# Moving the mixers' GpSimd element work, and one LN affine, to VectorE in a four-layer kernel

## The chip, the cores and the metric

The kernel runs on one core of one Trainium2 chip. A core has a matrix engine (TensorE, PE in the views; its weight loads are shown as PEld), three engines for element work (VectorE = DVE, ScalarE = ACT, GpSimd = POOL), and SyncE (SP), which here only issues transfers. The metric is the device time of one execution in microseconds (us), as a median of several runs. Each engine takes its instructions in order; an instruction that has to wait for another engine or a transfer holds up what stands behind it on its own engine.

## The reference

The input is 256 tokens of 1024 fp32 values. Two hybrid layers come first, then two blocks that each have a mixer and a mixture of experts (MoE). Cut to what matters:

```
def hybrid_layer(x, ...):                 # called twice
    p = rmsnorm(x, norm_g) @ w_in         # 3488 columns
    q, k, v   = low-rank attention inputs, rmsnorm per head, rope
    o_a       = causal attention(q, k, v)
    o_b       = c_b * short_conv(c_c * c_h, conv_w)
    o_c       = sg_u * (w_s @ layernorm(sg_v) + b_s)
    o_d       = second causal attention, rmsnorm per head, rope
    y = concat([o_a*silu(g_a), o_b*silu(g_b), o_c*silu(g_c), o_d*silu(g_d)])
    return y @ w_out                      # added to x by the caller

def second_block(x, c, ...):
    for i in range(2):                    # i = 0: NA, i = 1: GQA
        sh1, sc1, g1, sh2, sc2, g2 = split(silu(c) @ ada_w[i] + ada_b[i])
        y = (neighbourhood_mixer, gqa_mixer)[i](x * (1 + sc1) + sh1)
        x = layer_norm(ALPHA * x + (1 + g1) * y, ln_g[i, 0], ln_b[i, 0])
        y = hierarchical_moe(x * (1 + sc2) + sh2)
        x = layer_norm(ALPHA * x + (1 + g2) * y, ln_g[i, 1], ln_b[i, 1])
    return x
```

## The kernel before

**Stages.** The program runs through hybrid layer 0, hybrid layer 1, the NA layer, the MoE of block 0, the GQA layer and the MoE of block 1. In the profiled execution these are about 0 to 165, 165 to 330, 330 to 495, 495 to 945, 945 to 1100 and 1100 to 1560.8 us. In the MoE stages weights stream through a ring of buffers; in the mixers (hybrid, NA, GQA) the weights are few and products many.

**Products in three.** A mixer's projection is not one fp32 product but three on values split in two parts (`mm3`, L177): each weight block is split by `split` (L117), per 128x1024 piece, into hi, a ScalarE copy (L125), and lo = v - hi (L128). In the kernel before, lo is made on VectorE or on GpSimd: every third piece goes to GpSimd by the string `SPLIT_ON_POOL`, and in two calls of `proj_wide`, the first projection of a hybrid layer (`wa`) and GQA's `wkv`, the parameter `e` sends the others there too. There are two halves of the hi and lo blocks, used in turn, so a piece can be split only when the products from two blocks earlier have read theirs.

**Row norms.** `rstd` (L180) makes 1/sqrt by a bit trick and three Newton steps. The scale (L191) and the seed (L192) are VectorE's; the steps (L194 to L202) are GpSimd's in a hybrid layer, 13 instructions, and VectorE's in GQA, 10 instructions, since there the last two of a step are one (L199). A hybrid layer calls it for `r3` (the low-rank inputs; L507 reads it), `rb` (the second attention's heads; L524), `rq` (the first attention's heads; L543 to L545) and `rv` (the spatial gate; L587).

**Other element work on GpSimd.** In a hybrid layer: a gain on the keys (L552), half of a gain (L569), the gate's gain, bias and mask (L588 to L590). In `mixer_out`, which closes NA and GQA: router weights (L787). In GQA: the rope tables (L903, 16 small ones) and the rope of the second half of the queries (`chain` with `e=G`, L931 to L938).

**The affine between the layers.** The MoE of block 0 ends with the normalised x; gain and bias of that layer norm are folded into GQA's input scale (`fold`), and x itself gets them later, by four instructions on 128x1024 (`affine`, L840), since `mixer_out` adds it to the mixer's output. They run on GpSimd behind the k and v projection; their rows come by transfer into block 6 early in the layer.

**The adaptive scales.** `ada_cols` computes silu(c) @ ada_w in 24 pieces, each a product of 16 instructions into a bank of its own (`pf`), a copy of that bank (L220 or L226, tile `parts`), a second small product, and a VectorE instruction (L723, tile `modc`). Pieces are put between the mixers' steps by `ADA_PLAN`, and TensorE cannot start the next before the last has been copied.

**What sets the order.** The program is written as a list of operations with tiles, and a list scheduler with a simulated timeline makes each engine's order from it. An edit to one operation can therefore move many.

## Time and profile before

| | |
|---|---|
| median of 3 runs | 1562.01 us (1561.87 to 1565.7) |
| span of the profiled execution | 1560.8 us |
| TensorE busy | 1231.1 us (79%) |
| VectorE busy | 569.4 us (36%), 1258 instructions |
| ScalarE busy | 356.6 us (23%) |
| GpSimd busy | 236.6 us (15%), 283 instructions |
| DMA, mean | 341 GB/s |

The shares are means over stages of two kinds. In the MoE stages the transfers run near 427 GB/s without a break and the element engines are nearly idle; in the mixers TensorE is 85% to 95% busy, and VectorE and GpSimd do most of their work there. So the mixers have to be read by stretches: the windows by stage first, then what TensorE waited for, then the timeline around each such wait.

### The profile page before, as it was taken

The page shows a single profiled execution, that of the slowest core. Times are in us where ns is not written, and L with a number is a line of the kernel's source. Part 1 is how long each engine was busy: PE and PEld are TensorE (multiplying, and loading weights), DVE is VectorE, ACT ScalarE, POOL GpSimd, SP SyncE. Part 2 cuts the span into 40 slices and gives each one's busy share as a digit, 9 for nine tenths or more (in the row PEclk, how much of TensorE's full clock was granted, in tenths as well). Part 3 has the DMA queues.
Part 4 walks back from the last instruction along what each step waited for, and adds up shares of the span by engine and source line. Part 5 has one row for each costly group of instructions (what it writes and reads, how often), then busy time and mean ns, then how long its engine had stood idle before and what let it go on. Part 6 is the DMA issues. An engine that isn't in the chain of part 4 may idle for free.

```text
span 1560.8 us, 24728 instructions
## 1 busy us (share of the span) xinstructions
PE 1231.1 (79%) x10584; PEld 789.8 (51%) x10584; DVE 569.4 (36%) x1258; ACT 356.6 (23%) x759; POOL 236.6 (15%) x283
## 2 busy tenths in 40 slices
PE   6898899999998986664877768889897764586774
PEld 6787788777967442321333326757543322243322
DVE  6677567555467210100111105877411100011113
ACT  5453443444442100000000004363100000010000
POOL 2721272122111200000000004320200000000000
PEclk9999999999999998876898889989999887798797
DMA  9436543468487999999999999575999999999995
GB/s 370 178 147 242 213 166 152 163 236 343 169 342 290 405 426 427 427 428 426 427 426 427 428 423 410 210 279 206 388 427 427 428 427 425 427 427 427 426 427 210
DMA packets 46705, 532.76 MB, mean 341 GB/s; under 512 B 7040, under 2 KB 10240, under 8 KB 15104
## 3 DMA queue, kind: packets, MB, share of 16 engines
q1 hardware_dynamic: 45440, 527.99, 82.2%
q10 hardware_dynamic: 1152, 3.15, 0.6%
q8 instruction: 85, 1.39, 0.4%
q14 instruction: 28, 0.23, 0.0%
HBM read 530.07 MB, written 1.05 MB: 340 GB/s over the span
## 4 chain that ended last, share of the span: by engine, by line
DMA 43%; PE 40%; DVE 9%; POOL 2%; ACT 2%; issue 2%; SPq 0%; DVEq 0%; ACTq 0%; POOLq 0%
DMA b<-in_moe_w_gate_up_dram 25%; DMA b<-in_moe_w_down_dram 16%; PE ps L162 14%; PE pd L177 9%; PE ps L177 8%; PE pf L162 3%; PE pd L162 3%; PE ps L159 3%; DMA b<-in_ada_w_dram 2%; DVE b L128 1%; ACT b L125 1%; POOL b L128 1%; POOL rs L196 0%; POOL rs L201 0%; DVE b L220 0%
## 5 line engine op out<-in xcount | busy, mean ns | idle before, releaser
L162 PE MATMUL ps<-b,b 128*32 128x256 f32 (+2 forms) x5248 | 484.6, 475 | 198.2 <-DMA b<-in_moe_w_gate_up_dram 138.9
L162 PEld LDWEIGHTS ps<-b,b 128*32 128x32 f32 (+1 forms) x5248 | 191.6, 120 | 432.1 <-issue 275.7
L177 PE MATMUL ps<-b,b 128*128 128x256 f32 (+1 forms) x1464 | 198.8, 295 | 6.6 <-DVE gates L565 5.6
L177 PEld LDWEIGHTS ps<-b,b 128*128 128x128 f32 x1464 | 186.7, 195 | 17.1 <-DVE gates L565 6.1
L177 PE MATMUL pd<-b,b 128*128 128x256 f32 (+2 forms) x1152 | 188.3, 320 | 4.6 <-ACT b L600 1.3
L177 PEld LDWEIGHTS pd<-b,b 128*128 128x128 f32 x1152 | 162.0, 196 | 25.3 <-issue 4.4
L128 POOL TENSOR_TENSOR b<-b,b 128x1024 fp32r<-128x1024 f32 (+2 forms) x46 | 115.5, 2517 | 348.2 <-ACT b L125 348.2
L125 ACT CAST b<-b 128x1024 fp32r<-128x1024 f32 (+1 forms) x124 | 126.1, 1035 | 160.2 <-PE ps L177 71.7
L226 ACT COPY b<-ps 128x256 f32<-128x256 f32 (+1 forms) x81 | 36.0, 449 | 456.4 <-PE ps L162 308.2
L128 DVE TENSOR_TENSOR b<-b,b 128x1024 fp32r<-128x1024 f32 x78 | 115.9, 1490 | 62.1 <-ACT b L125 57.0
L220 DVE COPY b<-ps 128x256 f32<-128x256 f32 (+1 forms) x71 | 36.2, 510 | 263.1 <-PE ps L162 214.1
L1115 POOL TENSOR_TENSOR b<-b,g 128x128 f32<-128x128 f32 x64 | 23.6, 399 | 595.1 <-PE ps L159 548.7
L1097 DVE SCALAR_TENSOR_TENSOR sl<-sl,ps 128x128 f32<-128x128 f32 x64 | 18.4, 288 | 248.4 <-ACT sl L1096 248.4
L159 PE MATMUL ps<-cst,b 128*128 128x128 f32 (+1 forms) x404 | 77.5, 302 | 39.7 <-DVE b L220 17.5
L159 PEld LDWEIGHTS ps<-cst,b 128*128 128x128 f32 (+1 forms) x404 | 45.3, 147 | 105.2 <-DVE b L220 34.7
L162 PE MATMUL pd<-b 64*128 64x512 f32 (+1 forms) x384 | 82.6, 552 | 15.4 <-DVE b L1145 12.9
L1145 DVE TENSOR_TENSOR b<-ps,parts 128x512 f32<-128x512 f32 x32 | 22.1, 692 | 180.8 <-PE ps L162 179.9
L162 PEld LDWEIGHTS ps<-b,x 128*128 128x128 f32 x512 | 68.3, 218 | 21.9 <-issue 18.4
L162 PE MATMUL ps<-b,x 128*128 128x128 f32 x512 | 72.2, 305 | 3.8 <-issue 1.6
L1096 ACT ACTIVATE sl<-ps 128x128 f32<-128x128 f32 x64 | 17.8, 278 | 236.9 <-PE ps L159 236.9
L162 PE MATMUL pf<-b,cact 128*32 128x256 f32 x704 | 56.0, 428 | 13.5 <-DVE modc L723 4.9
L162 PEld LDWEIGHTS pd<-b 64*128 64x128 f32 x384 | 34.3, 190 | 52.9 <-DVE b L1145 26.2
(304 smaller groups left out, 944.0 us busy)
## 6 DMA issues: line engine op xcount, KB each, us to landing
b<-in_moe_w_gate_up_dram SPq DMA_DIRECT2D x128, 2048.0 KB, 32.5
b<-in_moe_w_down_dram SPq DMA_DIRECT2D x62, 2048.0 KB, 35.3
b<-in_ada_w_dram SPq DMA_DIRECT2D x24, 2048.0 KB, 8.4
b<-in_w_in_dram SPq DMA_DIRECT2D x12, 2048.0 KB, 8.0
b<-in_na_w_qkv_dram SPq DMA_DIRECT2D x6, 2048.0 KB, 9.3
b<-in_gqa_w_qkv_dram SPq DMA_DIRECT2D x3, 2048.0 KB, 23.4
b<-in_w_out_dram SPq DMA_DIRECT2D x4, 1024.0 KB, 5.7
b<-in_w_out_dram SPq DMA_DIRECT2D x2, 2048.0 KB, 7.4
```

Source lines behind the costliest of these rows:

```text
L125: S.copy(hi[:, s], v[:, s])
L128: (G if on_pool else e).tensor_tensor(lo[:, s], v[:, s], hi[:, s].bitcast(F32), OP.subtract)
L159: T.transpose(o, a, ident)
L162: return T.matmul(o, lhsT=a, rhs=b, start=start, stop=stop)
L177: T.matmul(o, lhsT=a[u], rhs=b[v], start=start and i == 0, stop=stop and i == 2)
L220: V.tensor_copy(o, i)
L226: S.copy(o, i)
L1096: S.activation(sl, ps[:, 0:128], AF.Tanh, scale=0.5)
L1097: V.scalar_tensor_tensor(sl, sl, 1.0, ps[:, 0:128], op0=OP.add, op1=OP.mult)
L1115: G.tensor_tensor(PG[:, t, :, du].rearrange("p q (e s) -> p q e s", e=2), P[:, t].rearrange("p (q e) s -> p q e s", q=2), g32[:, t, 4 * g: ...
L1145: V.tensor_tensor(do, ps, parts, OP.mult)
```

## The change

- `split` makes lo always on VectorE; `SPLIT_ON_POOL` and the parameter `e` of `split` and `proj_wide` go.
- `rstd` runs on VectorE everywhere, in its form with 10 instructions.
- The gains, bias and mask of the hybrid layer, the router weights, the rope tables and the rope of the second half of the queries move to VectorE.
- The affine between the layers moves from behind GQA's k and v projection, on GpSimd, into GQA's attention, on VectorE: two instructions after head pair 3 and two after head pair 5. Its rows now come into the part of block 10 that the rope used, so they are fetched only after the last rope. The affine inside each MoE stays on GpSimd.

The core of the diff:

```diff
@@ split
-        def split(v, e=V):
+        def split(v):
...
                 S.copy(hi[:, s], v[:, s])
-                par[1] += 1
-                on_pool = SPLIT_ON_POOL[par[1] % len(SPLIT_ON_POOL)] == "1"
-                (G if on_pool else e).tensor_tensor(lo[:, s], v[:, s], hi[:, s].bitcast(F32), OP.subtract)
+                V.tensor_tensor(lo[:, s], v[:, s], hi[:, s].bitcast(F32), OP.subtract)
@@ rstd
-        e = e or (G if len(big) < 11 else V)
+        e = V
@@ hybrid layer
-        pa = proj_wide(hT, split, wa, feed, G, ahead=ahead)
+        pa = proj_wide(hT, split, wa, feed, ahead=ahead)
...
-        G.tensor_tensor(kn[:, :, :, 0:64], kn[:, :, :, 0:64],
+        V.tensor_tensor(kn[:, :, :, 0:64], kn[:, :, :, 0:64],
...
-            (V, G)[q].tensor_tensor(bn[:, :, 4 * q:4 * q + 4], bn[:, :, 4 * q:4 * q + 4],
+            V.tensor_tensor(bn[:, :, 4 * q:4 * q + 4], bn[:, :, 4 * q:4 * q + 4],
...
-            G.tensor_tensor(vn[:, t], vn[:, t], rowl[:, R_SG:R_SG + 256], OP.mult)
-            G.tensor_tensor(vn[:, t], vn[:, t], rowl[:, R_SB:R_SB + 256], OP.add)
-        G.tensor_tensor(sgw, sgw, triu[:, None, :].to_broadcast([128, 4, 128]), OP.mult)
+            V.tensor_tensor(vn[:, t], vn[:, t], rowl[:, R_SG:R_SG + 256], OP.mult)
+            V.tensor_tensor(vn[:, t], vn[:, t], rowl[:, R_SB:R_SB + 256], OP.add)
+        V.tensor_tensor(sgw, sgw, triu[:, None, :].to_broadcast([128, 4, 128]), OP.mult)
@@ mixer_out
-            G.tensor_tensor(w, wge[0], c[:, :, None].to_broadcast([128, 8, 36]), OP.mult)
+            V.tensor_tensor(w, wge[0], c[:, :, None].to_broadcast([128, 8, 36]), OP.mult)
@@ affine
-    def affine(lgb):
-        for t in range(2):
+    def affine(lgb, e, ts=(0, 1)):
+        for t in ts:
             for i, op in enumerate((OP.mult, OP.add)):
-                G.tensor_tensor(x[:, t], x[:, t], lgb[i], op)
+                e.tensor_tensor(x[:, t], x[:, t], lgb[i], op)
@@ GQA layer
-        lgb = carve(block(6), (D,), (D,))
-        ln_rows(lgb, 0, 1)
...
-                    G.tensor_tensor(tab[:, qk, t, i], axc[:, t, j], gv[:, :, b], OP.mult)
+                    V.tensor_tensor(tab[:, qk, t, i], axc[:, t, j], gv[:, :, b], OP.mult)
...
-        pkv = proj_wide(hT, split, wkv, feed, G, rest)
+        pkv = proj_wide(hT, split, wkv, feed, rest)
         ada()
-        affine(lgb)
...
-        chain(pq, 8, 8, 0, G)
+        chain(pq, 8, 8, 0)
+        lgb = carve(b10[:, 1024:3072], (D,), (D,))
+        ln_rows(lgb, 0, 1)
...
             if hp == 1:
                 q_trans(1)
+            if hp in (3, 5):
+                affine(lgb, V, (hp // 4,))
@@ moe
-                affine(lgb)
+                affine(lgb, G)
```

**Where instructions stand.** GpSimd's list shrinks from 211 rows to 40, VectorE's grows from 1136 to 1272; TensorE's has the same instructions, with the low-rank query products (`uq`) and some adaptive pieces earlier or later. Line numbers of the changed kernel are 3 lower than those of the kernel before from `rstd` on (L128 is L125, L199 is L196, L524 is L521). A row is line, operation, output and inputs, and shape.

The Newton steps for `rb` in layer 0, on GpSimd, in the kernel before; the L128 between them is a split.

```order
L194 TENSOR_SCALAR rs<-rs 128x16
L196 TENSOR_TENSOR rs<-rb 128x16
L197 TENSOR_TENSOR rs<-rs 128x16
L128 TENSOR_TENSOR b_83<-b_669,b_82 128x1024
L201 TENSOR_SCALAR rs<-rs 128x16
L202 TENSOR_TENSOR rb<-rb,rs 128x16
```

The last of the three steps on VectorE in the changed kernel, the instruction that reads `rb`, and what follows it.

```order
L193 TENSOR_TENSOR rs<-rb 128x16
L194 TENSOR_TENSOR rs<-rs 128x16
L196 SCALAR_TENSOR_TENSOR rb<-rs,rb 128x16
L521 TENSOR_TENSOR b_87<-pd,rb 128x1024
L125 TENSOR_TENSOR b_83<-b_660,b_82 128x1024
L566 TENSOR_TENSOR b_87<-b_87,rowl 128x2x256 x2
```

The steps now stand in the list of the engine that uses their result, and the splits stand behind it.

VectorE at the start of the GQA layer, in the kernel before: statistics of the MoE's output and its normalisation (L775 writes x, which TensorE then transposes).

```order
L767 BN_AGGR lmv<-lst_7016 128x2
L211 TENSOR_SCALAR rsh<-lrr,rsh 128x1
L768 TENSOR_SCALAR lrr<-lmv 128x1
L212 TENSOR_SCALAR lrr<-rsh,lrr 128x1
L208 TENSOR_SCALAR lrr<-lrr 128x1
L209 TENSOR_SCALAR rsh<-lrr 128x1
```

The same place in the changed kernel (b_7012 is the lo half that the splits of `wkv` write).

```order
L764 BN_AGGR lmv<-lst_6992 128x2
L208 TENSOR_SCALAR rsh<-lrr,rsh 128x1
L125 TENSOR_TENSOR b_7012<-b_7031,b_7011 128x1024
L765 TENSOR_SCALAR lrr<-lmv 128x1
L209 TENSOR_SCALAR lrr<-rsh,lrr 128x1
L125 TENSOR_TENSOR b_7012<-b_7031,b_7011 128x1024
L205 TENSOR_SCALAR lrr<-lrr 128x1
L206 TENSOR_SCALAR rsh<-lrr 128x1
L208 TENSOR_SCALAR rsh<-lrr,rsh 128x1
L125 TENSOR_TENSOR b_7012<-b_7031,b_7011 128x1024 x2
```

Four splits, which GpSimd had here, now stand between the steps of the normalisation.

VectorE in GQA's attention in the changed kernel, where the affine (L837) now stands; L217 and L219 evacuate and scale attention weights, L349 is the row maximum of the next head pair.

```order
L846 TENSOR_TENSOR b_7618<-ps,b_7618 128x256
L219 TENSOR_SCALAR b_7619<-b_7619,sums 128x256 x2
L837 TENSOR_TENSOR x<-x,b_7014 128x1024 x3
L217 COPY b_7619<-ps 128x512
L837 TENSOR_TENSOR x<-x,b_7014 128x1024
L349 TENSOR_REDUCE mx<-pd 128x4 x2
```

All four stand close together, ahead of the two maxima. On SP's list the transfers of their rows moved from between two weight loads early in GQA to behind the last adaptive loads of the layer.

## Rows read from the trace of the kernel before

**Rows 1.** Windows, hybrid, GQA: us; busy PE, PEld, DVE, ACT, POOL; PEclk, DMA, GB/s.

```profile
0.00:330.00 330.00, 292.60 (x2168) 253.22 (x2172) 216.05 (x398) 147.02 (x276) 115.15 (x150) 0.96 0.56 208
...
945.00:1100.00 155.00, 132.59 (x1026) 102.61 (x1022) 118.05 (x293) 71.75 (x153) 44.27 (x27) 0.94 0.70 274
```

**Rows 2.** Waits of TensorE from 0 to 500: us, times, longest.

```profile
PE ps L159 <- DVE att L456: 15.0, 3, 9.7
...
PE ps L159 <- DVE x L809: 2.2, 2, 1.8
PE ps L162 <- DVE cv L653: 2.1, 1, 2.1
```

**Rows 3.** Groups of L128: busy us, mean ns; then ns min/median/max.

```profile
L128 POOL TENSOR_TENSOR b<-b,b 128x1024 fp32r<-128x1024 f32 x42 | 108.2, 2579 | 347.5 <-ACT b L125 347.5
...
L128 DVE TENSOR_TENSOR b<-b,b 128x1024 fp32r<-128x1024 f32 x78 | 115.9, 1490 | 62.1 <-ACT b L125 57.0 <-DMA b<-in_ada_w_dram 4.8
...
L128 DVE TENSOR_TENSOR b<-b,b x78: 1207/1225/3453, 14.0 to 1076.0; 128x1024 fp32r<-128x1024 f32 x78
```

**Rows 4.** Timeline, layer 0: start us, us, engine, line; [idle before <-releaser].

```profile
48.01 0.41 DVE L507 SCALAR_TENSOR_TENSOR b<-pd,r,rowl 128x32 f32<-128x32 f32 x2 [1.58 <-POOL r L202]
...
51.34 3.39 POOL L128 TENSOR_TENSOR b<-b,b 128x1024 fp32r<-128x1024 f32 x1
...
57.80 1.23 DVE L524 TENSOR_TENSOR b<-pd,rb 128x1024 f32<-128x1024 f32 x1 [4.74 <-POOL rb L202]
...
71.47 0.18 DVE L543 TENSOR_TENSOR rq<-rq,r 128x16 f32<-128x16 f32 x1 [2.56 <-POOL rq L202]
...
75.75 2.46 DVE L270 TENSOR_TENSOR b<-b,sc 128x160 f32<-128x160 f32 x1
...
78.13 0.31 DVE L271 TENSOR_TENSOR b<-b,sc 128x160 f32<-128x160 f32 x1
...
78.83 1.51 PE L162 MATMUL pf<-b,cact 128*32 128x256 f32 x12 [4.76 <-DVE parts L220]
```

**Rows 5.** Windows in which TensorE's granted clock was half (PEclk 0.50).

```profile
76.60:83.40 6.80, 4.57 (x36) 2.38 (x37) 6.80 (x16) 0.41 (x1) 2.55 (x4) 0.50 0.57 243
...
233.60:240.40 6.80, 3.11 (x14) 3.11 (x15) 6.76 (x14) 0.41 (x1) 2.75 (x4) 0.50 0.42 148
...
278.00:284.80 6.80, 6.16 (x32) 5.83 (x33) 4.31 (x10) 4.26 (x15) 1.21 (x1) 0.50 0.55 178
...
991.40:994.80 3.40, 3.40 (x18) 3.40 (x18) 1.29 (x2) 0.75 (x1) 0.00 (x0) 0.51 0.04 14
```

**Rows 6.** Timeline, layer 1, the same places as in rows 4.

```profile
215.40 1.23 DVE L524 TENSOR_TENSOR b<-pd,rb 128x1024 f32<-128x1024 f32 x1 [5.00 <-POOL rb L202]
...
237.29 2.93 PE L177 MATMUL ps<-b,b 128*128 128x256 f32 x12 [5.63 <-DVE gates L565]
```

**Rows 7.** Timeline, the norm at the start of layer 1.

```profile
166.86 2.45 DVE L456 TENSOR_SCALAR att<-x,ss 128x1024 f32<-128x1024 f32 x1
```

**Rows 8.** Timeline, the start of GQA: copies for `wkv`, normalisation, transposes.

```profile
945.40 3.88 ACT L125 CAST b<-b 128x1024 fp32r<-128x1024 f32 x4 [12.27 <-DMA b<-in_gqa_w_qkv_dram]
...
951.79 1.53 DVE L775 TENSOR_SCALAR x<-pd,lmv,lrr 128x512 f32<-128x512 f32 x2 [0.22 <-ACT x L774]
...
953.90 1.53 PE L159 MATMUL ps<-cst,x 128*128 128x128 f32 x12
```

**Rows 9.** Timeline, the middle of GQA: splits on VectorE, TensorE's two waits.

```profile
967.00 9.58 DVE L128 TENSOR_TENSOR b<-b,b 128x1024 fp32r<-128x1024 f32 x3 [4.55 <-ACT b L125]
...
982.39 1.93 PE L162 MATMUL pf<-b,cact 128*32 128x256 f32 x32 [2.86 <-DVE modc L723]
...
986.05 2.71 DVE L937 TENSOR_TENSOR b<-b 128x128 f32<-128x128 f32 x2
...
991.16 0.88 PE L162 MATMUL pf<-cst,parts 128*128 128x2 f32 x4 [3.42 <-DVE parts L220]
```

**Rows 10.** Timeline, SP's queue: the last adaptive load of GQA.

```profile
1018.61 0.33 SPq L696 DMA_DIRECT2D b<-in_ada_w_dram  x1
```

More of the change, by code (lines that the diff above doesn't have):

```diff
@@ L114, in splitter @@
         hs, ls = block(3, F32R), block(4, F32R)
-        par = [0, 0]
-        def split(v, e=V):
+        par = [0]
+        def split(v):
             k, n = v.shape[1], v.shape[2]
@@ L316, in proj_feat, with proj_wide @@
         return ps.rearrange("p (f t) -> p f t", f=2)
-    def proj_wide(h, split, v, feed=None, e=V, rest=None, ahead=()):
+    def proj_wide(h, split, v, feed=None, rest=None, ahead=()):
         o = PS2()
@@ L326, in proj_wide @@
                     q.enter_context(tc.issue_after(i))
-                s = [(a, split(v[:, :, a:min(a + 256, v.shape[2])], V if ahead and not a else e))
+                s = [(a, split(v[:, :, a:min(a + 256, v.shape[2])]))
                      for a in range(0, v.shape[2], 256)]
@@ L893, in gqa_layer @@
         wq = p["gqa_w_qkv_2"][0]
-        lgb = carve(block(6), (D,), (D,))
-        ln_rows(lgb, 0, 1)
         qT, kT, qk_t = carve(block(8), (8, 256), (4, 256), (2, 8, 64))
-        kdup, qs, ro, tab, vv = carve(block(10), (2, 4, 2, 64), (2, 8, 64), (4, 8, 2, 16), (2, 2, 4, 2, 16), (2, 256))
+        b10 = block(10)
+        kdup, qs, ro, tab, vv = carve(b10, (2, 4, 2, 64), (2, 8, 64), (4, 8, 2, 16), (2, 2, 4, 2, 16), (2, 256))
         axc = cst[:, C_AX:C_AX + 128].rearrange("p (t j a r) -> p t j a r", t=2, j=2, a=2)
@@ L912, in gqa_layer, with chain @@
         rs8 = small([128, 16, 2], "rs8")
-        def chain(pw, h0, n, qk, e=V):
+        def chain(pw, h0, n, qk):
             pv = pw[:, :, :n * 64].rearrange("p t (h d) -> p t h d", h=n)
@@ L930, in chain @@
                 tm = [ro[:, i, :n] for i in range(4)]
-                e.tensor_tensor(tm[0], xv[:, :, :, 0], tb[0], OP.mult)
-                e.tensor_tensor(tm[1], xv[:, :, :, 1], tb[1], OP.mult)
-                e.tensor_tensor(tm[2], xv[:, :, :, 1], tb[2], OP.mult)
-                e.tensor_tensor(tm[3], xv[:, :, :, 0], tb[3], OP.mult)
+                V.tensor_tensor(tm[0], xv[:, :, :, 0], tb[0], OP.mult)
+                V.tensor_tensor(tm[1], xv[:, :, :, 1], tb[1], OP.mult)
+                V.tensor_tensor(tm[2], xv[:, :, :, 1], tb[2], OP.mult)
+                V.tensor_tensor(tm[3], xv[:, :, :, 0], tb[3], OP.mult)
                 for d in ([qk_t[:, t]] if qk == 0 else [kdup[:, t, :, dd] for dd in range(2)]):
                     d = d.rearrange("p h (a b r) -> p h a b r", a=2, b=2)
-                    e.tensor_tensor(d[:, :, :, 0], tm[0], tm[1], OP.subtract)
-                    e.tensor_tensor(d[:, :, :, 1], tm[2], tm[3], OP.add)
+                    V.tensor_tensor(d[:, :, :, 0], tm[0], tm[1], OP.subtract)
+                    V.tensor_tensor(d[:, :, :, 1], tm[2], tm[3], OP.add)
         def q_trans(half):
```

1 line of the change is left out of this document (removed).

## Prediction

> **What bounds the kernel now.** I read the windows by stage first [rows 1]. In the hybrid layers TensorE is busy 292.6 of 330 us, VectorE 216.1 and GpSimd 115.2; in GQA 132.6, 118.1 and 44.3 of 155. No element engine is full on average, so what it costs has to be read where TensorE stands. The two MoE stages run at the transfers' pace; their streams begin when the mixer ahead gives its buffers back, so I pass an earlier end of a mixer on to the end one for one. That is a choice: a stream that had started earlier already would pass on less.
>
> The list of waits [rows 2] says that TensorE's long ones in the first 500 us end with VectorE instructions: the norm at L456, x at L809, the convolution at L653, and, on the timeline, an adaptive product (L162) that waits 4.76 us for a copy [rows 4] and the same place of layer 1 with 5.63 us [rows 6]. GQA has 2.86 and 3.42 us [rows 9]. The question is why VectorE is late there, and the rows give two reasons.
>
> First, it waits for GpSimd. L507 stands 1.58 us, L524 4.74 us and L543 2.56 us for the Newton steps, since GpSimd has a split of 3.39 us between them [rows 4]; in layer 1 L524 waits 5.00 us [rows 6].
>
> Second, it is slowed while GpSimd runs. L270 took 2.46 us, its twin L271 0.31 us [rows 4]. A split on VectorE has a median of 1.225 us, but its mean is 1.490 and its longest 3.453 [rows 3]; three in GQA, beside the affine, took 9.58 us together [rows 9]. L456 took 2.45 us [rows 7]; unslowed it would be 0.31 by L270's ratio and 0.94 by that of the three splits, and I take 0.75, an estimate.
>
> **The change part by part.** The time is worked against the profiled span of 1560.8 us, 1.2 us under the median of 1562.0; I add that 1.2 at the end.
>
> What VectorE takes over: 42 splits of 128x1024 at 1.225 us are 51.5 us, and four smaller ones about 3; on GpSimd the 42 took 108.2 us [rows 3]. Six calls of the Newton steps with 10 instructions at 0.18 us (the row of L543, same shape [rows 4]) are 10.8. The affine is 4 x 1.225 = 4.9. Some 46 smaller instructions, between 0.18 us and half a split, are put at 0.3 each, 14. Sum 84 us. What VectorE gets back: 78 splits x (1.490 - 1.225) = 20.7 us [rows 3], two L270 at 2.15 each, and what other operations lose beside GpSimd. Of these I have only single rows, so the return has ends: 25 us if little else was slowed, 84 if every operation under GpSimd's 159 us of these two stages lost as L270 did. Nearest are the splits, which lose 18% on average over the whole mixer; the short operations lose more. I take 70, net 14 us more on VectorE over the mixers. So it isn't the sum that decides but where the 84 us stand.
>
> *Layer 0, up to the 4.76 us wait.* Between L507 (48.0) and the copy at 78.4, VectorE is rid of 1.58 + 4.74 + 2.56 = 8.9 us of waiting and of about 3.2 us of slowing (2.15 at L270, four splits at 0.265). It is given three splits (3.7), 30 Newton steps (5.4) and two gains of half a split's size (1.2), 10.3. If all of that lies on the path, the copy comes 1.8 us earlier; if much of it falls into VectorE's other gaps (it idles 114 of 330 us [rows 1], only a part of that for GpSimd), the whole 4.76 goes. I take -3.8, nearer that end because of those gaps.
>
> *Layer 1, the same place.* The same instructions, the same waits [rows 6], the gate L565 last; between -1.8 and -5.6, I take -3.4.
>
> *The smaller waits* [rows 2]. The convolution's 2.1 us come behind slowed operations: -1.5. L809 closes NA and stands slowed too: -0.8 of 2.2. The short waits of the attentions I put at as much in each layer, -0.8 and -0.8.
>
> *Start of layer 1.* L456 gives back 1.7 us [rows 7], but four splits of `wa` that GpSimd had now stand in VectorE's list ahead of the instructions that feed the first product. Of 4 x 1.225 = 4.9 us I put some 2.2 on the path, since the first products need only the piece that is split first; 2.2 - 1.7 = +0.5, between -1.7 (all hidden) and +3.2 (none).
>
> *Clock.* Behind four of these waits the granted clock is half, 1.2 instead of 2.4 GHz, for a stretch [rows 5]. TensorE's work in it would take half: 2.3, 1.6 and 3.1 us lost in the hybrid layers. Where TensorE no longer stood before, I expect full clock, but most of these waits shrink rather than vanish; I take half of 7.0, -3.5, ends 0 and -7.
>
> *Start of GQA.* This speaks against the change. ScalarE's copies for `wkv` are done one by one from 946.4 on [rows 8], the lo parts now stand on VectorE among the steps of the normalisation (the order of the changed kernel shows four there), and L775, which writes x, stands behind them. 4.9 us, less the 1.3 us that the first normalised token tile (952.6) lay ready before TensorE reached its transposes (953.9) [rows 8]: +3.5, and a half-clock stretch behind the longer wait, +1.5. Ends +2 and +6.5.
>
> *Middle of GQA.* The three splits of 9.58 us become 3.7, and one that GpSimd had between them adds 1.2: VectorE is 4.7 us earlier, more than the wait of 2.86. Ahead of the second wait two small rope instructions (L937) took 2.71 us together and should take about 0.6, while another split adds 1.2: with the 1.8 left over from the first wait that is 2.7 of the 3.42. In all -5.6; I take -6.3, both, since the short operations between them were slowed as well, and half of the 1.7 us that the clock behind costs [rows 5], -0.9. What is late next there is TensorE itself. Least: -3, if only the first goes.
>
> *Attention and affine.* The four instructions of 4.9 us now stand ahead of two row maxima on VectorE, with TensorE's next weights behind them. VectorE is idle 24% of this stage [rows 1], so I take +1, ends 0 and +4.9. Their transfers are issued behind the last adaptive load (1018.6 [rows 10]) and behind the last rope, and have to land before the sixth of eight head pairs; if they land later, VectorE stands with the maxima, copies and scalings of attention behind it. The rope of the second half, 12 instructions, also moves into this list, but no longer slows it: 0. Closing of GQA, as of NA: -0.8.
>
> Hybrid and NA: -3.8 - 3.4 - 1.5 - 0.8 - 0.8 - 0.8 + 0.5 - 3.5 = -14.1. GQA: +5.0 - 6.3 - 0.9 + 1.0 - 0.8 = -2.0. Together -16.1: a span of 1544.7 and a median of about **1546 us**, 1.0% less.
>
> **A rule against it.** VectorE is busy 216.1 of 330 us in the hybrid layers [rows 1], but 6.80 of 6.80 in the stretch around one of the long waits [rows 5]. On full engines the Trainium skill says (Perfetto Trace Analysis, section Optimizing Scalar/DVE Operations) that work may be offloaded from a saturated VectorE even to GpSimd, though the two share a read port, so that it might not help. By the first half this change goes the wrong way, and the time would be that of the third rival below; by the second it gets back what the forecast's 70 us stand for. The trace bears out the second where both run, with 2.46 against 0.31 us.
>
> **Rivals.**
> 1. *Stalls go, but the end gets half.* The clock stays where it was (0 instead of -3.5 and -0.9), and the starts of layer 1 and GQA cost their upper ends (+3.2, +6.5): -16.1 + 4.4 + 2.7 + 1.5 = -7.5, 1554.5 us. For it: those two places are plain in the order. Chance 0.17.
> 2. *All clock comes back,* and the two long hybrid waits go whole: -16.1 - 3.5 - 0.9 - 1.0 - 2.2 = -23.7, 1538 us. For it: the waits all have one cause. Chance 0.12.
> 3. *VectorE becomes the bound.* The return is 25 us instead of 70, so VectorE has 59 us more, in a list that is in order: each inserted split (1.2 us) also waits for its copy on ScalarE and holds up softmax, norm and copies behind it. If half of the 59 falls where TensorE waits for VectorE, +29.5, less the 13.9 us of waits for GpSimd that go (8.9 in layer 0, 5.0 in layer 1): +15.6, 1578 us. It decides where more than 14 us of the added work lie on the path. Against it: VectorE idles 114 of 330 us, and much of this was waiting. Chance 0.13.
> 4. *Nothing measurable.* The new waits at the norms and the affine equal those that go, or the streams of the MoE stages take the gain back: 1562 us. Chance 0.11. That the change doesn't do what it says I leave out: the order shows the instructions on VectorE.
>
> **How the numbers follow.** The forecast has 0.47. A measurement of this kernel can tell about 0.3%, 4.7 us, from no change. Forecast and rivals 1 and 2 lie beyond that: faster 0.76; same 0.11; slower 0.13. The range leaves rival 3 out, and a little of the second's far end: 1533 to 1563.
>
> **What would show it.** Right: in the changed profile the copy at layer 0's adaptive product is no longer awaited for over 1 us, splits on VectorE have a mean near 1.23 us, TensorE's waits around 980 and 991 are gone, and the start of GQA shows transposes 3 to 5 us later against the end of the MoE. Wrong: new waits of TensorE that end with L125 on VectorE, in the start of layer 1 above all; an affine that waits for its rows; splits that still take over 1.4 us with GpSimd idle, since then it was not GpSimd that slowed them; or a mixer that ends earlier by 10 us with an end that does not move.

## Result: 1542.15 us, and the profile after

The changed kernel runs in 1542.15 us (median of 4 runs, 1540.82 to 1542.62), the kernel before in 1563.86 us (4 runs beside it); the ratio is 0.9855 with a 95% interval of 0.9837 to 0.9873. The forecast was 1546, with a range of 1533 to 1563. The profiled span fell from 1560.8 to 1537.7 us, by 23.1; the medians differ by 21.7.

Where the 23.1 us went is read from the times at which VectorE finishes each stage: the last addition to x in a hybrid layer (L679 before, L676 after), the last L809 (L806) of `mixer_out`, and the first statistics (L766, L763) behind a MoE.

| stage, us | before | after | difference | forecast |
|---|---|---|---|---|
| hybrid layer 0 | 165.3 | 154.1 | -11.2 | -13.3 for both |
| hybrid layer 1 | 163.5 | 154.3 | -9.2 | (in the row above) |
| NA | 160.8 | 163.4 | +2.6 | -0.8 |
| MoE 0 | 456.2 | 456.1 | -0.1 | 0 |
| GQA | 145.5 | 140.1 | -5.4 | -2.0 |
| MoE 1 to the end | 469.5 | 469.7 | +0.2 | 0 |

The two MoE stages keep their length, so an earlier end of a mixer did pass on whole. These are the windows of the hybrid layers, NA and GQA in the changed kernel, with the columns of rows 1:

```profile
0.00:308.40 308.40, 286.03 (x2178) 249.69 (x2179) 224.35 (x519) 145.86 (x273) 0.20 (x4) 0.98 0.59 223
308.40:471.80 163.40, 151.31 (x1161) 124.82 (x1159) 105.81 (x198) 70.86 (x150) 0.00 (x0) 0.98 0.68 260
927.90:1068.00 140.10, 123.33 (x968) 93.98 (x964) 108.42 (x273) 67.38 (x147) 0.00 (x0) 0.96 0.69 275
```

and the same stages of the kernel before, cut at its own stage ends:

```profile
0.00:328.80 328.80, 291.42 (x2152) 252.61 (x2152) 214.85 (x398) 146.56 (x275) 114.18 (x150) 0.96 0.56 209
328.80:489.60 160.80, 154.02 (x1185) 124.69 (x1184) 100.80 (x187) 70.28 (x148) 26.83 (x12) 0.97 0.68 265
945.80:1091.30 145.50, 125.18 (x968) 96.02 (x964) 110.05 (x246) 69.33 (x148) 44.27 (x27) 0.94 0.68 267
```

GpSimd had 185.3 us of work in the three (114.18 + 26.83 + 44.27) and now has 0.2. VectorE's busy time rose from 425.7 to 438.6 us, by 12.9 only, although it took over work that the prediction put at 84 us; by that estimate 71 us came back. Counted on single instructions it is 63: in the three stages of the kernel before, 46 instructions of VectorE took over 0.15 us more than the same operation takes in the changed kernel, 63.1 us together. In GQA the busy time even fell, with 27 more instructions. The groups of splits in the whole program, and two others, show where part of it came from (before: rows 3, 4 and 7):

```profile
L125 DVE TENSOR_TENSOR b<-b,b 128x1024 fp32r<-128x1024 f32 x120 | 145.5, 1220 | 65.9 <-ACT b L124 64.6
...
L453 DVE TENSOR_SCALAR att<-x,ss 128x1024 f32<-128x1024 f32 x4 | 3.0, 749 | 0.1
...
L267 DVE TENSOR_TENSOR b<-b,sc 128x160 f32<-128x160 f32 x2 | 0.6, 314 | 0.0
```

A split now takes 1.220 us, mean and median alike (1.490 before); L453 is L456, 0.749 us now against 2.45 in rows 7; L267 is L270, 0.31 against 2.46 in rows 4.

The timeline at TensorE's two long hybrid waits, of layer 0 (4.76 us, rows 4) and layer 1 (5.63 us, rows 6), and, second fence, at the start of layer 1:

```profile
73.07 1.93 PE L159 MATMUL pf<-b,cact 128*32 128x256 f32 x32 [0.52 <-DVE parts L217]
...
233.31 2.42 PE L174 MATMUL ps<-b,b 128*128 128x256 f32 x18 [0.23 <-ACT qT L223]
```

```profile
155.74 0.75 DVE L453 TENSOR_SCALAR att<-x,ss 128x1024 f32<-128x1024 f32 x1
156.41 3.83 DVE L125 TENSOR_TENSOR b<-b,b 128x1024 fp32r<-128x1024 f32 x4
156.64 1.59 PE L156 MATMUL ps<-cst,att 128*128 128x128 f32 x8 [2.41 <-DVE att L453]
...
160.67 7.53 PE L174 MATMUL pd<-b,b 128*128 128x256 f32 x33 [2.23 <-DVE b L468]
```

Both long waits are down to half a microsecond or less. At the start of layer 1 the norm takes 0.75 us, and four splits, 3.83 us, now stand between it and L468, which makes the lo part of the first product: 4.10 us of waiting have become 2.41 + 2.23.

At the start of GQA (rows 8 before) the splits stand in the normalisation:

```profile
927.91 1.29 DVE L763 BATCH_NORM_STATS2 lst<-pd 128x6 f32<-128x512 f32 x2 [1.23 <-PE pd L159]
...
931.19 1.22 DVE L125 TENSOR_TENSOR b<-b,b 128x1024 fp32r<-128x1024 f32 x1
...
932.52 1.21 DVE L125 TENSOR_TENSOR b<-b,b 128x1024 fp32r<-128x1024 f32 x1
...
933.96 2.35 DVE L125 TENSOR_TENSOR b<-b,b 128x1024 fp32r<-128x1024 f32 x2
...
938.38 1.53 DVE L772 TENSOR_SCALAR x<-pd,lmv,lrr 128x512 f32<-128x512 f32 x2 [0.22 <-ACT x L771]
939.24 2.82 PE L156 MATMUL ps<-cst,x 128*128 128x128 f32 x12 [5.45 <-DVE x L772]
```

x is begun 10.5 us behind the first statistics; before it was 6.0 (945.8 to 951.79).

### The profile page after: what moved, and what is told of

Read it like the earlier page. It is cut to its first block, busy times and chain, and to the rows that moved or that the text cites. A ratio compares the mean times of both kernels' runs of the same rounds, so it can differ in the third digit from the quotient of the medians.

```text
span 1537.7 us, 24637 instructions
## 1 busy us (share of the span) xinstructions
PE 1221.9 (79%) x10584; PEld 788.6 (51%) x10584; DVE 585.8 (38%) x1434; ACT 355.9 (23%) x759; POOL 48.1 (3%) x83
## 3 DMA queue, kind: packets, MB, share of 16 engines
q8 instruction: 85, 1.39, 0.4%
HBM read 530.07 MB, written 1.05 MB: 345 GB/s over the span
## 4 chain that ended last, share of the span: by engine, by line
DMA 46%; PE 43%; DVE 8%; ACT 2%; issue 1%; SPq 0%; DVEq 0%; ACTq 0%
DMA b<-in_moe_w_gate_up_dram 25%; DMA b<-in_moe_w_down_dram 19%; PE ps L159 13%; PE pd L174 11%; PE ps L174 11%; PE pd L159 3%; PE pf L159 2%; PE ps L156 2%; DVE b L125 2%; DMA b<-in_na_bias_dram 1%; ACT b L124 1%; DMA b<-in_ada_w_dram 1%; DMA b<-in_w_in_dram 0%; DVE b L217 0%; DVE mx L349 0%
## 5 line engine op out<-in xcount | busy, mean ns | idle before, releaser
L174 PE MATMUL ps<-b,b 128*128 128x256 f32 (+1 forms) x1464 | 194.9, 292 | 0.8 <-DVE ch L217 0.5
L174 PEld LDWEIGHTS pd<-b,b 128*128 128x128 f32 x1152 | 163.5, 198 | 29.2 <-DVE b L468 5.9
L125 DVE TENSOR_TENSOR b<-b,b 128x1024 fp32r<-128x1024 f32 (+1 forms) x124 | 148.6, 1207 | 65.9 <-ACT b L124 64.6
L217 DVE COPY b<-ps 128x256 f32<-128x256 f32 (+1 forms) x71 | 36.0, 507 | 260.6 <-PE ps L159 216.6
L159 PE MATMUL pd<-b 64*128 64x512 f32 (+1 forms) x384 | 83.1, 551 | 14.6 <-DVE b L1144 11.3
L227 ACT ACTIVATE b<-ps,modc 128x128 f32<-128x128 f32 x64 | 29.0, 457 | 130.7 <-DVE b L221 77.5
L221 DVE TENSOR_SCALAR b<-ps,modc 128x128 f32<-128x128 f32 x64 | 25.8, 408 | 80.1 <-ACT b L227 41.9
```

Source lines behind the costliest of these rows:

```text
L125: V.tensor_tensor(lo[:, s], v[:, s], hi[:, s].bitcast(F32), OP.subtract)
L159: return T.matmul(o, lhsT=a, rhs=b, start=start, stop=stop)
L174: T.matmul(o, lhsT=a[u], rhs=b[v], start=start and i == 0, stop=stop and i == 2)
L217: V.tensor_copy(o, i)
L221: V.tensor_scalar(o, i, scale, bias, op0=OP.mult, op1=OP.add)
L227: S.activation(o, i, AF.Identity, scale=scale, bias=bias)
```

## Experiments

Theory A, that of the prediction, has two causes of about equal weight: VectorE waited for GpSimd's Newton steps, and VectorE was slowed while GpSimd ran. B says the waits alone, C the slowing alone. (In the prediction itself the weights differ: on the way to layer 0's long wait it has 8.9 us of waiting and about 3.2 of slowing.) For each kernel the table gives the stages of one profiled execution, read as above; hybrid is the end of layer 1. The diffs show the core of each edit, with "..." where lines are left out.

| kernel | hybrid | NA | GQA | span | ratio to before (95%) |
|---|---|---|---|---|---|
| before | 328.8 | 160.8 | 145.5 | 1560.8 | 1 |
| changed | 308.4 | 163.4 | 140.1 | 1537.7 | 0.9855 (0.9837 to 0.9873) |
| e1 Newton steps alone | 321.6 | 161.9 | 151.9 | 1559.9 | 0.9981 (0.9964 to 0.9998) |
| e2 splits alone | 311.3 | 165.3 | 141.6 | 1543.9 | 0.9873 (0.9856 to 0.9889) |
| e3 affine back | 309.8 | 163.8 | 142.8 | 1542.7 | 0.9862 (0.9846 to 0.9879) |
| e4 wkv splits back | 307.1 | 163.5 | 136.8 | 1533.3 | 0.9826 (0.981 to 0.9843) |
| e5 idle work on GpSimd | 324.7 | 164.0 | 143.5 | 1558.3 | 0.9964 (0.9949 to 0.998) |
| e6 a third of NA's splits back | 309.5 | 160.8 | 141.5 | 1536.3 | 0.9834 (0.9807 to 0.9862) |
| e7 e4 and e6 together | 309.5 | 160.6 | 141.7 | 1537.1 | 0.9846 (0.9822 to 0.9869) |
| e8 half of wa in layer 1 back | 309.1 | 165.4 | 140.0 | 1541.6 | 0.9867 (0.9839 to 0.9895) |
| e9 idle work, one element | 309.2 | 163.4 | 140.1 | 1538.5 | 0.9848 (0.9829 to 0.9868) |
| e10 wkv splits behind the norm | 310.1 | 163.4 | 140.9 | 1539.5 | 0.9848 (0.9832 to 0.9865) |
| e11 all splits back | 322.3 | 162.6 | 138.1 | 1548.5 | 0.9895 (0.9873 to 0.9917) |
| e12 splits moved in hybrid only | 309.8 | 161.7 | 138.8 | 1534.0 | 0.983 (0.9813 to 0.9847) |

**How far a stage's time can be trusted.** e4 has the order of the changed kernel, instruction for instruction, through both hybrid layers, yet its layers 0 and 1 take 155.3 and 151.8 us against 154.1 and 154.3: 1 to 2.5 us is what one execution differs from another there. Where the scheduler makes another order the difference is larger: e7 has e4's edit in GQA, but another order there on TensorE, VectorE and ScalarE, and takes 141.7 against 136.8. So a stage difference under 5 us is read only where several kernels agree, or where the timeline shows its place.

### Newton steps alone, splits alone

```diff
-        e = e or (G if len(big) < 11 else V)
+        e = V
```

> The kernel before with one part of the change: the Newton steps of the hybrid layers on VectorE; splits, gains and affine stay on GpSimd. The changed kernel ends the two hybrid layers 20.4 us earlier (308.4 against 328.8). Theory A (two causes of about equal weight: waits for GpSimd's Newton steps, and VectorE slowed beside GpSimd): the waits of 1.58, 4.74 and 2.56 us in layer 0 and their likes in layer 1 go, the slowing stays: the hybrid layers end 6 to 11 us earlier, total 1551 to 1557. Theory B (it is the waits for GpSimd alone): 17 us or more earlier, total near 1544. Theory C (it is the slowing alone): under 3 us, total 1559 or more.

```diff
-SPLIT_ON_POOL = "010"
+SPLIT_ON_POOL = "000"
...
-split(v[:, :, a:min(a + 256, v.shape[2])], V if ahead and not a else e))
+split(v[:, :, a:min(a + 256, v.shape[2])], V))
```

> The kernel before with one part of the change: all splits on VectorE; Newton steps, gains, rope half and affine stay on GpSimd. Theory A: the slowing under the 2.58 us splits goes in hybrid and GQA, and with no split in its list GpSimd does its Newton steps without the break of 3.39 us, so part of the waits goes as well: hybrid 8 to 13 us earlier, GQA 2 to 5, total 1545 to 1552. Theory B: hybrid under 5 us earlier. Theory C: hybrid 17 us or more, total near 1541.

The Newton steps alone end the hybrid layers 7.2 us earlier, theory A's value (6 to 11), although the total stays at theory C's (1560.6). The splits alone end them 17.5 us earlier, theory C's value (17 or more), with a total of 1545.05 at the near end of A's. Both with the gains bring 20.4. So B falls. The two overlap, since with the splits gone GpSimd does its Newton steps at once. VectorE's waits for GpSimd in the hybrid layers of the kernel before and, second fence, with the splits alone moved (engine, tile and line, who it waited for: us, times, longest):

```profile
DVE b L524 <- POOL rb L202: 9.7, 2, 5.0
...
DVE rq L543 <- POOL rq L202: 5.1, 2, 2.6
DVE b L507 <- POOL r L202: 4.0, 2, 2.4
```

```profile
DVE vn L587 <- POOL rv L202: 3.0, 2, 2.4
DVE b L524 <- POOL rb L202: 1.9, 2, 1.2
DVE rq L543 <- POOL rq L202: 1.4, 1, 1.4
DVE b L507 <- POOL r L202: 1.0, 1, 1.0
```

18.8 us become 7.3 with the steps still on GpSimd. What had made them late was mostly the splits in GpSimd's queue. The slowing is seen on single instructions of VectorE in the hybrid layers, those over 0.15 us longer than the same operation in the changed kernel: 24 before (36.6 us lost together), 10 with the splits alone moved (some 7 us), but 29 with the Newton steps alone moved (43.6 us). So e1 removes 18.8 us of waiting and adds 7.0 us of slowing. At TensorE's two long waits, 4.76 and 5.63 us before, e1 leaves 2.19 and 3.24 us, e2 1.89 and 0.99: neither cause alone makes them.

e1 also shows a cost outside its edit: GQA takes 151.9 us, 6.4 more, though nothing of GQA was edited. TensorE has new waits there (3.84 us for L938, 2.07 for a softmax of ScalarE, 1.88 for a copy), in an order that came out differently. That is why e1 gains 0.2% in all and not the 0.5% of its hybrid layers.

### Work on GpSimd that nobody reads

To part the slowing from the queue, I put GpSimd's splits back as idle work: after VectorE has made lo, GpSimd subtracts hi once more from the weights, which are not read any more. In the control it does so on one element per partition. (`third_or_wa` stands for the condition that the kernel before splits this piece on GpSimd.)

```diff
                 V.tensor_tensor(lo[:, s], v[:, s], hi[:, s].bitcast(F32), OP.subtract)
+                third_or_wa and G.tensor_tensor(v[:, s], v[:, s], hi[:, s].bitcast(F32), OP.subtract)   # e5
+                third_or_wa and G.tensor_tensor(v[:, a, 0:1], v[:, a, 0:1], hi[:, a, 0:1].bitcast(F32), OP.subtract)   # e9
```

> The changed kernel, with work added on GpSimd in the hybrid layers whose result nothing reads: for each piece that the kernel before split on GpSimd there, GpSimd subtracts hi from the weights once more, in place, after VectorE has made lo. It holds the weights' buffer about as long as before and runs beside VectorE, but no engine waits for its value. The hybrid layers end at 308.4 us in the changed kernel, 311.3 with the splits alone moved, 328.8 before. Theory C (VectorE slowed beside GpSimd is what the moved splits had cost): splits on VectorE get a mean of about 1.4 to 1.5 us, L268 to L270's likes over 1 us again, hybrid ends at 319 or later. Theory B' (it is the place in GpSimd's queue and its slower subtract that others waited for): VectorE's instructions are slowed, but the hybrid layers end before 313. Theory A: between.

> Control for e5: the same instructions on GpSimd at the same places with the same readers and buffers, but on one element per partition in place of 1024, so that they take some 0.2 us each in place of 2.6. Orders of the engines stay close to those of e5 (42 lines apart on TensorE, 30 on VectorE). e5 ended the hybrid layers at 324.7 us, the changed kernel at 308.4. Theory C (VectorE slowed beside GpSimd's long operations): 307 to 312. Rival (the added instructions, their order or the later release of the weights' buffers cost it): 318 or later.

The windows of the hybrid layers, e5 first:

```profile
0.00:324.70 324.70, 291.51 (x2177) 255.10 (x2178) 252.57 (x519) 146.05 (x273) 64.64 (x30) 0.96 0.56 211
```

```profile
0.00:309.00 309.00, 285.89 (x2176) 249.50 (x2177) 224.27 (x518) 145.87 (x273) 11.36 (x30) 0.98 0.59 222
```

The instructions on VectorE are the same (519 and 518 in the window); beside 64.6 us of long GpSimd work they take 252.6 us, beside 11.4 us of short work 224.3. That is 28.3 us of slowing, and the hybrid layers end 15.5 us later. No engine waits for the value. The transfers that refill the weights' buffers do wait until GpSimd has read them, but no engine stands more than 0.2 us longer for a transfer: ScalarE waits 2.2 us for weights in e5 and in e9, TensorE 0.2 us in e5 and not at all in e9. In e5 TensorE's long waits come back in part without a wait of VectorE for GpSimd (2.64 us for `parts` in layer 0, 1.98 for the gate in layer 1, 3.50 + 4.02 at the start of layer 1). The groups of VectorE in e5's hybrid layers:

```profile
L125 DVE TENSOR_TENSOR b<-b,b 128x1024 fp32r<-128x1024 f32 x71 | 95.7, 1357 | 19.3 <-ACT b L124 19.2
L453 DVE TENSOR_SCALAR att<-x,ss 128x1024 f32<-128x1024 f32 x4 | 4.8, 1210 | 0.1
L125 DVE TENSOR_TENSOR b<-b,b 128x960 fp32r<-128x960 f32 x2 | 4.4, 2220 | 0.0
L267 DVE TENSOR_TENSOR b<-b,sc 128x160 f32<-128x160 f32 x2 | 2.8, 1391 | 0.0
```

On average splits take 1.357 us instead of 1.221 in e9, the 960-column ones 2.22 instead of 1.15, L267 1.39 instead of 0.32. The averages hide the form. Of the 519 instructions 18 are over 0.15 us longer than in e9, 30 us together (6 of the 71 splits and one of the two L267 among them), and the others take what they take there. Each of the 18 begins while a GpSimd subtract runs, and ends 0.03 to 1.1 us behind its end; L267 of layer 1, 0.32 us in e9:

```profile
231.46 2.54 POOL L125 TENSOR_TENSOR b<-b,b 128x1024 f32<-128x1024 f32 x1 [10.67 <-DVE b L125]
231.71 2.47 DVE L267 TENSOR_TENSOR b<-b,sc 128x160 f32<-128x160 f32 x1
```

So C is a cause by itself: 15.5 us against e9, where the change gained 20.4. The idle work runs behind VectorE's lo and not in its place, so it does not fall on quite the same instructions as the splits of the kernel before. The Newton steps' waits add a part of their own, e1, but were late mostly through the same splits. A was right that both exist and, over the hybrid layers, wrong on equal weight. The Trainium skill (SBUF — State Buffer, section Who interferes with whom) says that a VectorE instruction with two SBUF inputs and a GpSimd one that reads SBUF contend, and that the one issued second waits; the trace of e5 agrees, with L267 begun 0.25 us behind the start of the GpSimd subtract and ended 0.18 us behind its end. The size here is 0.44 us of VectorE for each microsecond of long GpSimd work (28.3 / 64.6), and that is no rate of slowing: it tells how often a VectorE instruction ran into a GpSimd one.

### All splits back

```diff
-                V.tensor_tensor(lo[:, s], v[:, s], hi[:, s].bitcast(F32), OP.subtract)
+                par[1] += 1
+                on_pool = SPLIT_ON_POOL[par[1] % len(SPLIT_ON_POOL)] == "1"
+                (G if on_pool else e).tensor_tensor(lo[:, s], v[:, s], hi[:, s].bitcast(F32), OP.subtract)
...
+        pa = proj_wide(hT, split, wa, feed, G, ahead=ahead)
...
+        pkv = proj_wide(hT, split, wkv, feed, G, rest)
```

> The changed kernel with the splits back where the kernel before had them (every third and the wa and wkv ones on GpSimd); Newton steps, gains, rope half and affine stay on VectorE. By the runs so far the splits alone brought 17.5 of the 20.4 us of the hybrid layers and the Newton steps alone 7.2. If the splits are the cause: the hybrid layers end at 319 to 326 us and the total is 1553 to 1562. Rival (once the other work is off GpSimd its splits are harmless): 308 to 314 and 1540 to 1547.

Hybrid 322.3, inside the range for the splits as the cause; the total, 1547.9, lies under its range, because GQA (138.1) and NA (162.6) are no longer than with all splits on VectorE. The windows of the hybrid layers and of NA:

```profile
0.00:322.30 322.30, 291.23 (x2184) 253.78 (x2184) 234.70 (x492) 146.75 (x275) 65.26 (x32) 0.97 0.57 215
322.30:484.90 162.60, 153.22 (x1154) 125.70 (x1152) 100.01 (x189) 70.29 (x148) 23.38 (x10) 0.96 0.67 259
```

In the hybrid layers VectorE is rid of 27 instructions (492 against 519), most of them splits, and is busier for it: 234.7 us against 224.35. What GpSimd took off it, some 32 us, it gave back and 10 more in slowing. In NA the same move makes VectorE less busy, 100.0 against 105.81.

### Start of layer 1

```diff
-        pa = proj_wide(hT, split, wa, feed, ahead=ahead)
+        pa = proj_wide(hT, split, wa, feed, G if l else V, ahead=ahead)
```

> The changed kernel with the splits of the first projection of hybrid layer 1 back on GpSimd (two of its four; the first two stay on VectorE by the parameter of that call), nothing else. TensorE waits 2.4 us for the norm (L453) and 2.2 us for the lo part behind it (L468) there, and a half-clock stretch of 10.2 us follows. If the splits in VectorE's list cost that: layer 1 150 to 153 us instead of 154.3. If GpSimd beside the norm gives it back: 154 to 156 us.

Layer 1 takes 154.5 us, the rival's value. GpSimd runs beside the norm again and lengthens it (0.75 to 1.89 us), so that TensorE waits longer for it and less for L468, 3.54 + 1.07 us instead of 2.41 + 2.23:

```profile
155.32 3.47 POOL L125 TENSOR_TENSOR b<-b,b 128x960 fp32r<-128x960 f32 x2 [154.87 <-ACT b L124]
156.18 1.89 DVE L453 TENSOR_SCALAR att<-x,ss 128x1024 f32<-128x1024 f32 x1
158.22 1.94 PE L156 MATMUL ps<-cst,att 128*128 128x128 f32 x8 [3.54 <-DVE att L453]
```

### Start of GQA

```diff
-        pkv = proj_wide(hT, split, wkv, feed, rest)
+        pkv = proj_wide(hT, split, wkv, feed, G, rest)
```

> The changed kernel with the four splits of GQA's k and v weights back on GpSimd, nothing else. In the changed kernel TensorE waits 5.5 us for x (L772), with these four splits (4.8 us) among the normalisation's steps. Theory A: the wait falls to about 1 to 2 us and the half-clock stretch behind it shortens: GQA 135 to 137.5 us instead of 140.1, total 1538 to 1540. Rival (GpSimd beside the normalisation slows it as much, or what is late next is the four splits themselves at 2.3 us each): GQA 139 to 142 us.

e10 leaves the four splits on VectorE and orders them behind the instruction that writes x:

```diff
-                V.tensor_tensor(lo[:, s], v[:, s], hi[:, s].bitcast(F32), OP.subtract)
+                with ExitStack() as q:
+                    if late[1]:
+                        q.enter_context(tc.issue_after(late[0].ins))
+                    V.tensor_tensor(lo[:, s], v[:, s], hi[:, s].bitcast(F32), OP.subtract)
```

`late[0]` is the instruction that writes the second token tile of x (L772, here L775), and `late[1]` is set for `wkv` alone.

> The changed kernel with the four wkv splits still on VectorE, but ordered behind the normalisation that writes x. In the changed kernel x was written at 938.4, 10.5 us behind the first statistics, and TensorE waited 5.5 us for it; with the splits on GpSimd 6.0 us behind them. Theory E (only the place in the list costs): x at 6 us, GQA 135 to 138 us as with the splits on GpSimd (136.8). Theory F (VectorE's load costs there: the four splits now hold up the scaling of the transposed x instead): x at 6 us, but GQA 139 to 142.

e4's GQA takes 136.8 us, theory A's value, with a total under its range. In both kernels x is begun 6.0 us behind the first statistics, as before the change. e4's timeline, then e10's:

```profile
926.07 9.27 POOL L125 TENSOR_TENSOR b<-b,b 128x1024 fp32r<-128x1024 f32 x4 [96.81 <-ACT b L124]
932.81 1.53 DVE L772 TENSOR_SCALAR x<-pd,lmv,lrr 128x512 f32<-128x512 f32 x2 [0.22 <-ACT x L771]
...
939.35 5.87 PE L174 MATMUL pd<-b,b 128*128 128x256 f32 x47
```

```profile
935.99 1.53 DVE L775 TENSOR_SCALAR x<-pd,lmv,lrr 128x512 f32<-128x512 f32 x2 [0.22 <-ACT x L774]
...
937.44 4.62 DVE L128 TENSOR_TENSOR b<-b,b 128x1024 fp32r<-128x1024 f32 x4
...
941.98 0.72 DVE L224 TENSOR_SCALAR b<-ps,fs,fb 128x128 f32<-128x128 f32 x2
```

In e4 the first product starts 12.5 us behind the first statistics (926.8 to 939.35), in the changed kernel 15.7 (927.9 to 943.65). In e10 the splits, 4.62 us, now hold up the scaling of the transposed x (L224, 941.98), the first product starts 14.75 us behind the statistics, and GQA takes 140.9: theory F. So most of the cost is VectorE's load at this place, and only 1.0 of the 3.2 us is the place in its list; GpSimd, beside the normalisation's 128x1 steps, did not make x later than e10 has it. The other kernels agree on the first product: 11.3 to 13.1 us where these splits are on GpSimd (before, e1, e4, e7, e11, e12), 14.75 to 15.75 where they are on VectorE (the changed kernel and the other seven). The wait of TensorE in e4 is no shorter than in the changed kernel (6.04 us), because an adaptive product that stood ahead of it now stands behind. What the 3 us at the first product are worth for the whole of GQA is open: e7 has them too, and its GQA takes 141.7.

### The affine

```diff
+        lgb = carve(block(6), (D,), (D,))
+        ln_rows(lgb, 0, 1)
...
+        affine(lgb, G)
...
-            if hp in (3, 5):
-                affine(lgb, V, (hp // 4,))
```

> The changed kernel with one part undone: the affine between the layers back on GpSimd behind GQA's k and v projection, its rows fetched early. In the changed kernel GQA takes 140.1 us between the first statistics and the last, before 145.5. Theory A (the affine slowed the splits beside it, 9.58 us for three): the splits behind the k and v projection take 3 us each again and the waits of about 2.9 and 3.4 us return in part, GQA 143 to 146 us. Rival (the affine costs more in the attention than it did there, 4.9 us on VectorE): GQA 136 to 140 us.

GQA 142.8, just under theory A's range, but above the rival's. The splits beside the affine were slowed less than before: 6.57 us for four, 1.64 each, not 3.2, since in this order only the first of them met GpSimd's 10.02 us:

```profile
949.55 10.02 POOL L837 TENSOR_TENSOR x<-x,b 128x1024 f32<-128x1024 f32 x4 [117.74 <-DMA b<-in_ln_g_dram]
957.49 6.57 DVE L125 TENSOR_TENSOR b<-b,b 128x1024 fp32r<-128x1024 f32 x4 [4.87 <-ACT b L124]
```

With 2.7 us, inside what an order can do, the affine's share isn't settled. What the changed kernel's trace shows is that it found its rows in time and took 1.2 us an instruction:

```profile
1010.37 0.61 DVE L219 TENSOR_SCALAR b<-b,sums 128x256 f32<-128x256 f32 x2
1010.89 3.49 DVE L837 TENSOR_TENSOR x<-x,b 128x1024 f32<-128x1024 f32 x3
1014.29 0.68 DVE L217 COPY b<-ps 128x512 f32<-128x512 f32 x1
1014.89 1.22 DVE L837 TENSOR_TENSOR x<-x,b 128x1024 f32<-128x1024 f32 x1
```

### NA, and a better mixture

```diff
-                V.tensor_tensor(lo[:, s], v[:, s], hi[:, s].bitcast(F32), OP.subtract)
+                par[1] += 1; (G if e is G or ghost[0] and "010"[par[1] % 3] == "1" else V).tensor_tensor(lo[:, s], v[:, s], hi[:, s].bitcast(F32), OP.subtract)
```

Here `ghost[0]` is 1 in the NA layer alone; e7 gives `wkv` the engine G as well.

> The changed kernel with every third split of the NA layer back on GpSimd, nothing else. NA takes 163.4 us in the changed kernel, 165.3 with the splits alone moved, 160.8 before. Theory D (in NA VectorE is the late one, and GpSimd's ten splits were a relief): NA falls to 160 to 162 us, total 1539 to 1541. Rival (the 2.6 us come from the changed order or from a load that lands later): NA stays at 163 to 165 us.

> The changed kernel with the four wkv splits of GQA on GpSimd and every third split of NA there too. If the two places are independent: GQA 136 to 138 us, NA as in the run with NA's third alone, total 1534 to 1537 if NA gains, 1537 to 1540 if not. If GpSimd's work in NA slows VectorE as it did in the hybrid layers, NA 164 us or more and a total above 1539.

In e6 and e7 NA takes 160.8 and 160.6 us, theory D, against 163.4 to 165.4 in the eight kernels that have all of NA's splits on VectorE; the six with every third on GpSimd (before, e1, e6, e7, e11, e12) have 160.6 to 162.6. The window of e6's NA:

```profile
309.50:470.30 160.80, 150.32 (x1154) 124.23 (x1152) 99.96 (x189) 70.11 (x148) 23.41 (x10) 0.98 0.68 264
```

VectorE's busy time is 99.96 us with GpSimd's 23.41 beside it, and 105.81 without. Of VectorE's 19 splits that begin in this stage five ran into one of GpSimd's and are lengthened, by 3.9 us together; that is 0.17 us for each microsecond of GpSimd against 0.44 in e5, and the relief is 5.9 net. e6 gives NA's time back, but not by all of the same waits: TensorE stands idle for 6.8 us of NA before, 12.1 in the changed kernel (3.1 for adaptive copies, 2.1 for L877) and 10.5 in e6 (2.7 for adaptive copies, none for L877). In GQA e7 gains nothing (141.7, expected 136 to 138), so the total, 1540.5, misses its 1534 to 1537, and the two reliefs together are no better than either.

e12 moves the splits in the hybrid layers alone:

> The changed kernel with its splits on VectorE in the hybrid layers alone: in NA and GQA every third one, and GQA's four wkv ones, are back on GpSimd; Newton steps, gains, rope half and affine stay on VectorE. The hybrid layers should end at 308 to 310 as in the changed kernel, NA take 160.7 us as with its third on GpSimd (160.8 and 160.6), GQA 138 us as in the run with all splits back (138.1). If the move pays in the hybrid layers alone: span 1532 to 1536, total 1534 to 1538, below the changed kernel's 1542. Rival (GQA's part is worth as much on VectorE, or its order falls out differently): GQA 140 to 143, total 1538 to 1543.

1536.94 us, 0.983 of before, inside its range, though NA (161.7) gave 1 us less and GQA (138.8) 1 less than hoped. e12 and e4 (1536.83) are about 5 us under the changed kernel; their intervals just touch its own (0.9847 and 0.9843 against 0.9837), so they are probably, not certainly, faster. Both are faster than the kernel before.

## Why the prediction was right, and where its steps were off

**As a whole.** The direction was right and the time lies in the range, but that range reached from 1533 to no change at all. The size was too small. 1546 against the 1562.0 that the prediction started from is 1.0% less; the measured ratio, 0.9855, would be 1539.4 from there (1540.3 by the difference of the medians), nearer to the 1538 of the second rival, which had a chance of 0.12, than to the forecast. The span says the same: -16.1 forecast, -23.7 by that rival, -23.1 measured, and in the hybrid layers -13.3, -20.0 and -20.4. By stage the forecast missed 7.1 us of gain in the hybrid layers, 3.4 in GQA, and 3.4 of loss in NA; that the last two cancel is luck.

**The sum on VectorE**: net 14 us were forecast (84 taken over, 70 given back) and 12.9 measured. The choice between 25 and 84 was made well, and the third rival, which needed 25, falls. That the net came out so near is partly luck. A hybrid layer calls `rstd` four times, so there are eight calls of the Newton steps and not six (14.4 us by the same price, not 10.8); the return is 63 us by the single instructions, not 70; and with 63 back and 12.9 net the work taken over costs some 76 us of busy time, less than the sum of its instructions, since neighbours overlap (four splits of 1.22 us take 4.62 in a row).

**Layer 0 and 1, the long waits.** -3.8 and -3.4 were forecast; the waits fell from 4.76 to 0.52 and from 5.63 to 0.23, which is -4.2 and -5.4. Layer 1 was undersized: its term stood below the middle of its range (-1.8 to -5.6), and the wait went whole. The two reasons named for these waits both hold (e1, e2, e5), but they are not apart: the steps were late because of the splits in GpSimd's queue.

**Clock.** Half of 7.0 was forecast. In layer 0 TensorE's clock stays full from 20.5 us to the end of the layer. In layer 1 the stretches at 233.6 and 278.0 (rows 5) are gone, one of 3.4 us has come at 262.8, and the one at the start of the layer has grown from 6.8 us (from 168.7) to 10.2 (from 157.0). (The one at 278.0 had stood behind two short waits of the attention, 0.59 and 1.43 us, not behind one of the long ones.) By the windows above TensorE's busy time in the hybrid layers fell by 5.4 us (291.4 to 286.0), mostly the clock's part, and its idle time by 15.0, where -3.5 for the clock and -9.8 for the waits were forecast. So the hybrid layers gave 20.4 us and not 13.3: the terms for the clock and for layer 1 were too small, the convolution's 2.1 us went whole, and some 2 us are in no term.

**Start of layer 1**, +0.5: 4.10 us of waits became 4.64, right to the size; that the half-clock stretch there would grow was not in the sum.

**NA**, -0.8, was wrong in sign: +2.6. The step that failed is the one that looked only at NA's closing L806, whose wait did not change, and did not count NA's ten splits as work added to VectorE there: it gained 5.0 us of busy time (100.80 to 105.81). In the kernel before only four instructions of NA had been lengthened, by 6.0 us, and the ten splits cost VectorE 12.2. e6 gives the time back; through which wait of TensorE is not settled.

**Start of GQA**, +5.0: x comes 4.5 us later against the statistics, as worked out, and the half-clock stretch there is 10.2 us (from 931.8), before 3.4 (from 950.4). **Middle of GQA**, -6.3 and -0.9: neither wait of rows 9 exists any more, splits take 1.22 us each. **Affine**, +1: no wait of TensorE names it; not settled finer. **Closing of NA and GQA**, -0.8 each: 0; TensorE's waits for L809 (L806) are 2.2 us at each, before and after.

**The rope of the second half** was put at 0 ("no longer slows it"), and by the timelines this is the term that GQA's forecast lacked, though no run moves the rope alone. In the kernel before, GpSimd did it from 1013.7 to 1022.0. There the Newton steps beside it took up to 0.78 us instead of 0.17, TensorE stood for 1.82, 1.05 and 1.78 us, and then ran at half clock for 10.2 us:

```profile
1014.00:1022.10 8.10, 3.86 (x48) 1.99 (x44) 7.93 (x14) 2.31 (x9) 7.97 (x12) 1.00 0.96 401
1022.10:1032.30 10.20, 9.14 (x40) 5.96 (x44) 5.14 (x12) 8.47 (x27) 0.00 (x0) 0.50 0.65 278
```

e1 and e2, which keep the rope on GpSimd, have 3.25 and 2.83 us of waiting at its end and 10.2 and 6.8 us at half clock. The changed kernel has full clock from 942.1 to the end of GQA, and no wait over 1.4 us between its first product and the wait that closes the stage.

**The rule against it.** The Trainium skill's two halves (Perfetto Trace Analysis, section Optimizing Scalar/DVE Operations) hold in different stages: in the hybrid layers the offload did not help, 234.7 us of VectorE with it (e11) and 224.35 without, and in NA it did, 100.0 against 105.81.

**Passing on.** The mixers gave 23.2 us (20.4 - 2.6 + 5.4) and the end 23.1: one for one.

## What to carry to other kernels

Work given to a second element engine is free only if the first isn't slowed by it: compare an operation's mean with its median, and a slow instance with its twin, and look whether the first engine's busy time in the stage falls at all. Decide it by stage: in the hybrid layers giving the splits to GpSimd made VectorE 10 us busier and the stage 13.9 us longer (e11), in NA it made VectorE 5.9 us less busy and the stage 2.6 shorter (e6). And under a scheduler that makes the order, an edit in one stage can cost 6 us in another (e1), so read a result by stage and trust a stage's few microseconds only when several kernels agree.
